# Encoder step on one core: last attention values earlier, output weights split over the first output rows, first two pairs of the up stage by turns

## The chip, the core and the metric

One Trainium2 chip, one core. The metric is the device time of one execution in microseconds. Each kernel is timed several times on a chip and the median is taken. A profiled execution gives a trace of every instruction beside it.

## What is computed

One inference step of a one-layer encoder. 1024 prompt positions and 8 samples of 16 positions make 1152 rows of width 1024, all in float32. In short:

```python
h = rmsnorm(x, g_pre_mix)
qa, ka, va, qb, kb, vb, ga, gb = project(h, w_in)
...
merged = jax.nn.sigmoid(ga) * (oa @ w_oa) + jax.nn.sigmoid(gb) * (ob @ w_ob)
x = x + rmsnorm(merged @ w_out, g_post_mix)
f, conv_new = conv_ffn(rmsnorm(x, g_pre_ffn), conv_buf, w_upg, conv_w, conv_b, w_down)
x = x + rmsnorm(f, g_post_ffn)
```

`oa` and `ob` are two windowed attentions. `conv_ffn` multiplies by `w_upg` (the up projection, 2 x 3072 columns), runs a causal convolution of width 3 and a GELU over one half, multiplies by the other half and by `w_down`.

## The kernel before, in words

Each float32 matrix product is made of three reduced-precision ones: an operand is split into a high part (a copy with rounding, on ACT) and a low part (the difference, on DVE or POOL), and high x high, high x low and low x high are summed in PSUM. An operand's high part is so ready before its low part, and PE can start on it with the matmuls that need the high part alone.

The program is a sequence of stages on PE: projections (0 to 297 us of the span), attention with the remaining projection columns spread between its steps (297 to 601), merge of the two branches with `w_o` (601 to 706), output projection `w_out` with both norms (706 to 816), up stage (816 to 1366), down stage (1372 to the end). The order of the work within a stage is that of the code, moved by a scheduler that places instructions by priority as their inputs become ready; a pool of `bufs=n` buffers makes the next tile wait for the last reader of the tile that had its place. Each engine then runs its own list in order, and SP's list issues the DMAs.

**End of attention** (L840 to L882). Column blocks of the projection are cut in pieces of four steps, a step being 6 matmuls ("dense", L117 to L119, tiles d). What is left at the end runs around the last transposes and `values(prev)`, the last product of attention with V, whose result goes through `oo` and DRAM to the merge's operands `oT` (L901 loads, L902 ACT's high part, L903 DVE's low part). The merge's first matmul is mp (L926). Its result per group g of columns is merged on DVE (L937, mm), split on ACT (L938, mT0h to mT2h) and POOL (L939).

**Output projection** (L985 on). Eight weight tiles wt0 to wt7 are split (L101 ACT, L104 DVE). Nine blocks of 128 rows follow in the order 8, 0 to 7. A block is 48 matmuls (L1060 to L1062, r), then norm, residual and norm (L1068 to L1075, result h), and transposes into the up stage's right operands (L1044 tp, copied out at L1050 or L1048). The blocks' transposes are kept in a list `pending` and run two blocks late; two are left at the end.

**Up stage** (L143 products; right operands xob, xot). 24 pairs f of a column block of the first half and one of the second. It is a scheme with seven products per pair instead of eight; a product is two chunks of 12 matmuls of 128x288, 24 in all, accumulated in a pair of banks x, y or z. For the first five pairs two of the seven products run ahead ("away", banks xh): h11 with right operand b11, then h12 with b21. The left operands come from the raw weights uw by sums on DVE (L127 to L133) and `split_left` (L1019 ACT, L1020 DVE; tiles a, s, h). `split_left` counts its calls with `turn`, 0 to 167, and takes one of two pools by the count:

```python
sp = (wop[1] if next(turn) % 3 else wop[0]).tile([P, 2, 4, P], F32R, name=name, tag="wop")
```

Pool wopa has one buffer and wopb two, so three buffers are used in rotation. ACT also copies results out of PSUM (L1110, L1158), DVE adds and runs the convolution (L1184 to L1220, L1197 the taps), POOL makes the last products (L1216, L1221), and SP stores them to z_dr (L1217, L1218, L1222, L1223).

**Down stage.** Its raw operands z12r, z14r, z16r (L1295, from z_dr) and wd12r and so on (L1296) take places that the up stage leaves. They are split at L1304 (ACT, zap, zs, wbp) and L1305 (DVE). The first matmul is p20s at L1366.

Of the kernel before, what the change touches and what calls it, by code (L numbers as in the profile page):

```python
# [11 lines left out]
F32 = mybir.dt.float32  # L12
# [6 lines left out]
P = 128  # L19
# [33 lines left out]
def encoder_step(ctx, tc, x, w_in, w_o, w_out, w_upg, w_down, kc, vc, state_conv, conv_w, conv_b,  # L53
# [23 lines left out]
    def bcast_row(pool, vec, n, name):  # L77
        t = pool.tile([P, n], F32, name=name)
        nc.sync.dma_start(t[:], bass.AP(tensor=vec.tensor, offset=vec.offset, ap=[[0, P], [1, n]]))
        return t  # L80
# [69 lines left out]
    def banks(pool, name):  # L150
        return [pool.tile([P, 512], F32, name=f"{name}_{c}", tag="ps")[:, 0:CW] for c in range(2)]
# [8 lines left out]
    with ExitStack() as ph:  # L160
# [61 lines left out]
        class Away:  # L222
# [9 lines left out]
            def run(self, i, c):  # L232
                if i == 0:
                    self.ps[c] = self.pool.tile([P, 512], F32, name=f"ixh{self.f}_{c}", tag="ps")[:, 0:CW]
                order = ((0, 0), (1, 0), (0, 1)) if self.early else ((0, 0), (0, 1), (1, 0))
                chunk_product(self.ps[c], self.left[i], of(rf[("b11", "b21")[i]]), c, i == 0, i == 1, order)
# [252 lines left out]
    with ExitStack() as ph:  # L489
# [347 lines left out]
        for u in range(8):  # L837
# [36 lines left out]
                prev = st  # L874
            for _ in dense:
                pass
        run(pieces[0])
        for _ in transposes(prev):
            pass
        run(pieces[1])  # L880
        values(prev)
        run(*pieces[2:])  # L882
    xk_stack.close()
    r1 = [r1_stack.enter_context(tc.tile_pool(name=f"r1{i}", bufs=1, reuse_waits="tile")) for i in range(4)]
    r2 = r2_stack.enter_context(tc.tile_pool(name="r2", bufs=2, reuse_waits="tile"))
# [99 lines left out]
    with ExitStack() as ph:  # L985
        psr = ph.enter_context(tc.tile_pool(name="psr3", bufs=3, space=PSUM, reuse_waits="tile"))
        pst = ph.enter_context(tc.tile_pool(name="pst3", bufs=2, space=PSUM, reuse_waits="tile"))
        xp = ph.enter_context(tc.tile_pool(name="xp3", bufs=2, reuse_waits="tile"))
        gp = ph.enter_context(tc.tile_pool(name="gp3", bufs=1, reuse_waits="tile"))
        gpm = bcast_row(gp, g_post_mix, D, "gpm")  # L990
        gpf = bcast_row(gp, g_pre_ffn, D, "gpf")
        gp.tile([P, 768], F32, name="gap")
        wp = ph.enter_context(tc.tile_pool(name="wp3", bufs=1, reuse_waits="tile"))
        wo = [wp.tile([P, 2, D], F32R, name=f"wt{k}") for k in reversed(range(KD))][::-1]
        for k in range(KD):
            raw = (wr if k % 4 > 1 else wr2).tile([P, D], F32, name=f"wt{k}r", tag="wr")
            nc.sync.dma_start(raw[:], w_out[k])
            split_w(raw, wo[k], "scalar", "vector")
        wr_stack.close()
        uraw = xo_stack.enter_context(tc.tile_pool(name="uraw", bufs=2, side="right", reuse_waits="tile"))  # L1000
        operand("b11")
        wop_a = xo_stack.enter_context(tc.tile_pool(name="wopa", bufs=1, side="right", reuse_waits="tile"))
        wop = [wop_a]

        bq = [[None, None], [None, None]]
        for h, q in ((0, 0), (0, 1), (1, 0), (1, 1)):
            bq[h][q] = r1[2 * h + q].tile([P, 2, 4, CW], F32, name=f"bq{h}{q}", tag="act")

        def up_weights(f, n=2):
            raw = uraw.tile([P, 2, KD, P], F32, name=f"uw{f}{n}", tag="uw")  # L1010
            for i in range(n):
                nc.sync.dma_start(raw[:, i], w_upg[i * NF + f])
            return raw

        turn = iter(range(7 * NF + 2 * NH))

        def split_left(src, name):
            sp = (wop[1] if next(turn) % 3 else wop[0]).tile([P, 2, 4, P], F32R, name=name, tag="wop")
            nc.scalar.activation(sp[:, 0], src, AF.Copy)  # L1019
            nc.vector.tensor_tensor(sp[:, 1], src, fr(sp[:, 0]), op=ALU.subtract)  # L1020
            return sp

        uraws = {f: up_weights(f, 1) for f in range(2)}
        early_op = {}

        def pieces(tb):

            t0, h = (tb * P, 0) if tb < NT - 1 else (H1, 0)
            done = 0
            while done < P:  # L1030
                t = t0 + done
                if tb < NT - 1 and t >= H1:
                    h, t = 1, t - H1
                n = min(P - done, CW - t % CW)
                if tb < NT - 1 and h == 0:
                    n = min(n, H1 - t)
                yield done, h, t // CW, t % CW, n
                done += n

        def transpose_block(src, tb):  # L1040
            for q in range(2):
                pt = pst.tile([P, 4, P], F32, name=f"tp{tb}_{q}", tag="pt")
                for k in range(4):
                    nc.tensor.transpose(pt[:, k], src[:, (4 * q + k) * P:(4 * q + k + 1) * P], ident[:])  # L1044
                for r, h, c, c0, n in pieces(tb):
                    dst = bq[h][q][:, c, :, c0:c0 + n]
                    if q and i < 7:
                        nc.vector.tensor_copy(dst, pt[:, :, r:r + n])  # L1048
                    else:
                        nc.scalar.activation(dst, pt[:, :, r:r + n], AF.Copy)  # L1050

        pending = []
        for i, tb in enumerate(order):
            g, c = tb // 3, (tb % 3) * P
            ps = psr.tile([P, 2, 512], F32, name=f"r{tb}", tag="r")
            for k in range(KD):
                mh, ml = mT[g][0][:, k, c:c + P], mT[g][1][:, k, c:c + P]
                for h in range(2):
                    hs = slice(h * 512, (h + 1) * 512)
                    nc.tensor.matmul(ps[:, h], mh, wo[k][:, 0, hs], start=k == 0, stop=False)  # L1060
                    nc.tensor.matmul(ps[:, h], mh, wo[k][:, 1, hs], start=False, stop=False)
                    nc.tensor.matmul(ps[:, h], ml, wo[k][:, 0, hs], start=False, stop=k == KD - 1)  # L1062
            xt = xp.tile([P, D], F32, name=f"xr{tb}", tag="xt")
            nc.sync.dma_start(xt[:], x[tb])
            st = xp.tile([P, 4], F32, name=f"str{tb}", tag="st")
            r2v = ps[:].rearrange("p a b -> p (a b)")
            h2 = xp.tile([P, D], F32, name=f"h2{tb}", tag="h2", bufs=3)
            nc.scalar.activation(h2[:], r2v, AF.Square, accum_out=st[:, 0:1])  # L1068
            rstd_of(st[:, 0:1], st[:, 1:2])
            nc.vector.scalar_tensor_tensor(h2[:], r2v, st[:, 1:2], gpm[:], op0=ALU.mult, op1=ALU.mult)  # L1070
            nc.vector.tensor_tensor(xt[:], xt[:], h2[:], op=ALU.add)
            nc.sync.dma_start(x1_dr[tb][:], xt[:])
            nc.scalar.activation(h2[:], xt[:], AF.Square, accum_out=st[:, 2:3])
            rstd_of(st[:, 2:3], st[:, 3:4])
            nc.vector.scalar_tensor_tensor(h2[:], xt[:], st[:, 3:4], gpf[:], op0=ALU.mult, op1=ALU.mult)  # L1075
            pending.append((h2, tb))
            while i >= 3 and len(pending) > 2:
                transpose_block(*pending.pop(0))
            if i == 6:
                for c in range(2):  # L1080
                    split_chunk("b11", bq[0][0], c, nc.vector)
                early_op[0] = split_left(uraws[0][:, 0, 0:4], "h11_0")
        for p in pending:
            transpose_block(*p)
    r2_stack.close()


    (b11, b21), (b12, b22) = bq
    wop.append(xo_stack.enter_context(tc.tile_pool(name="wopb", bufs=2, side="right", reuse_waits="tile")))
    pa = xo_stack.enter_context(tc.tile_pool(name="pa", bufs=4, side="right", reuse_waits="tile"))  # L1090
    for name in ("b21", "t3", "t2", "t1", "b22", "t4"):
        operand(name)
# [3 lines left out]
    with ExitStack() as ph:  # L1096
# [23 lines left out]
            product(yb, next(ops), of("b21"), True, True)  # L1120
            return ops, xb, a, yb

        def head_away(f):

            raw = uraws.pop(f, None) or up_weights(f, 1)
            xb = banks(psx, f"xh{f}")
            product(xb, early_op.pop(f, None) or split_left(raw[:, 0, 0:4], f"h11_{f}"), of("b11"), True, False)
            a = snap(xb, [pa.tile([P, CW], F32, name=f"ah{f}_{c}", tag="a")[:] for c in range(2)])
            for c in range(2):
                nc.sync.dma_start(a_dr[f][:, c], a[c])  # L1130
            product(xb, split_left(raw[:, 0, 4:8], f"h12_{f}"), of("b21"), False, True)
            o = [pa.tile([P, CW], F32, name=f"ch{f}_{c}", tag="a") for c in range(2)]
            snap(xb, [t[:] for t in o])
            for c in range(2):
                nc.sync.dma_start(c_dr[f][:, c], o[c][:])

        def head_back(f):
            a = [pa.tile([P, CW], F32, name=f"a{f}_{c}", tag="a")[:] for c in range(2)]
# [111 lines left out]
        forms = right_factors()  # L1250
        next(forms)
        for f in range(NH):
            head_away(f)
            if f in (1, 2):
                next(forms)
        for f in range(NF):
# [323 lines left out]
```

## Time and profile before

| | us |
|---|---|
| median of 3 runs | 1643.92 (1643.70 to 1643.96) |
| profiled execution | 1648.29 |
| its span in the trace | 1646.5 |
| stage r, 706 to 816.3 | 110.3 |
| start of the up stage, 816.3 to 855 | 38.7 |
| rest of the up stage, 855 to 1360 | 505.0 |

The span runs from the first to the last instruction of the trace; the profiled execution's time is 1.8 us longer and 4.4 us over the median. Engines: PE matmuls, PEld weight loads (beside PE), DVE, ACT, POOL, SP (DMA issues). In a row of the timeline stand the start, the duration of the group, engine, line, operation, out<-in, shape and count, and in brackets the idle time before it and what ended that. Names have no buffer numbers there. A group's matmuls overlap, so its duration is a little longer than its share of the pitch.

### The profile page before, as it was taken

The numbers are of one execution on the slowest core, as the hardware profiler recorded it, in microseconds if no ns is written. First come the engines' busy times: TensorE is split into PE (matmuls) and PEld (weight loads), VectorE is DVE, ScalarE is ACT, GpSimd is POOL, SyncE is SP. The second block draws the span as 40 slices with busy tenths as digits, with TensorE's granted clock in tenths as the row PEclk, the third lists the DMA queues.
The fourth block names the chain that finished last, engine by engine and source line by source line (L and its number), as shares of the span: only waits on it lengthen the run. The fifth ranks groups of instructions, "written<-read, shape, count | busy, mean of one in ns | idle before, by whom it ended". The sixth has DMA issues, their size and how long they took to land. (4 is left out here: it accounts for less than half of the span.)

```text
span 1646.5 us, 27860 instructions
## 1 busy us (share of the span) xinstructions
PE 1591.7 (97%) x10887; PEld 1471.5 (89%) x10887; DVE 1096.0 (67%) x2015; ACT 726.1 (44%) x1411; POOL 215.9 (13%) x293
## 2 busy tenths in 40 slices
PE   6999999999999999999999999999999998999997
PEld 5999999878788889978799999999999997888886
DVE  6965544677777746353597866667666665966986
ACT  7611233566555544332373344444444444534342
POOL 1000000221110004310002311122111110000004
PEclk9999999999999999999999999999999999999999
DMA  7743321664543155342164312212212228053023
GB/s 257 250 166 136 119 95 73 215 183 146 167 152 102 60 198 183 120 166 90 67 205 139 106 66 81 69 67 81 81 66 81 75 80 314 1 215 110 1 100 130
DMA packets 93636, 206.47 MB, mean 125 GB/s; under 512 B 19464, under 2 KB 43320, under 8 KB 93504
## 3 DMA queue, kind: packets, MB, share of 16 engines
q1 hardware_dynamic: 93504, 204.69, 36.4%
q8 instruction: 85, 1.39, 0.3%
q14 instruction: 47, 0.39, 0.1%
HBM read 148.13 MB, written 61.24 MB: 127 GB/s over the span
## 5 line engine op out<-in xcount | busy, mean ns | idle before, releaser
L143 PE MATMUL x<-xot,s 128*128 128x288 f32 x1152 | 157.7, 295 | 1.5 <-DVE w L1156 1.5
L143 PEld LDWEIGHTS x<-xot,s 128*128 128x128 f32 x1152 | 154.9, 188 | 1.7 <-ACT a L1019 1.7
L1366 PE MATMUL x<-wbp,zap 128*128 128x512 f32 x576 | 135.3, 389 | 0.0
L1366 PEld LDWEIGHTS x<-wbp,zap 128*128 128x128 f32 x576 | 108.1, 188 | 22.5
L1366 PE MATMUL p<-wbp,zap 128*128 128x512 f32 x432 | 102.4, 394 | 0.0
L1019 ACT ACTIVATE s<-uw 128x512 fp32r<-128x512 f32 x96 | 60.1, 627 | 94.6 <-issue 42.0
L671 ACT ACTIVATE p<-p,m 128x256 f32<-128x256 f32 (+4 forms) x128 | 74.8, 586 | 56.5 <-DVE m L666 56.5
L1366 PEld LDWEIGHTS p<-wbp,zap 128*128 128x128 f32 x432 | 82.4, 191 | 17.3
L1020 DVE TENSOR_TENSOR s<-uw,s 128x512 fp32r<-128x512 f32 x96 | 70.1, 730 | 34.0 <-ACT s L1019 34.0
L1197 DVE SCALAR_TENSOR_TENSOR wk<-w,cw,wk 128x128 f32<-128x128 f32 (+2 forms) x144 | 83.2, 614 | 7.4 <-ACT wk L1195 6.6
L1020 DVE TENSOR_TENSOR a<-uw,a 128x512 fp32r<-128x512 f32 x62 | 42.9, 693 | 63.3 <-ACT a L1019 62.0
L143 PE MATMUL x<-xob,s 128*128 128x288 f32 x576 | 81.1, 295 | 3.2 <-ACT wk L1195 1.4
L143 PEld LDWEIGHTS x<-xob,s 128*128 128x128 f32 x576 | 78.1, 188 | 3.8 <-ACT wk L1195 1.6
L143 PE MATMUL z<-xot,s 128*128 128x288 f32 x576 | 80.7, 295 | 0.0
L143 PE MATMUL z<-xot,a 128*128 128x288 f32 x576 | 80.7, 295 | 0.0
L143 PE MATMUL ix<-t,s_i 128*128 128x288 f32 x576 | 78.6, 295 | 0.3 <-DVE iu L188 0.3
L143 PEld LDWEIGHTS z<-xot,s 128*128 128x128 f32 x576 | 78.1, 188 | 0.0
L143 PEld LDWEIGHTS z<-xot,a 128*128 128x128 f32 x576 | 78.1, 188 | 0.0
L143 PEld LDWEIGHTS ix<-t,s_i 128*128 128x128 f32 x576 | 77.2, 188 | 0.5 <-issue 0.5
L173 ACT ACTIVATE s_i<-iw 128x512 fp32r<-128x512 f32 x48 | 30.3, 630 | 88.4 <-PE ix L143 49.0
L143 PE MATMUL x<-xob,a 128*128 128x288 f32 x456 | 63.9, 295 | 0.0
L143 PE MATMUL y<-xob,a 128*128 128x288 f32 x456 | 63.9, 295 | 0.0
(625 smaller groups left out, 3828.2 us busy)
## 6 DMA issues: line engine op xcount, KB each, us to landing
uw<-in_w_upg SPq DMA_DIRECT2D x53, 512.0 KB, 4.4
iw<-in_w_in SPq DMA_DIRECT2D x31, 512.0 KB, 4.6
gg<-in_dr SPq DMA_DIRECT2D x16, 576.0 KB, 3.7
z_dr<-wk SPq DMA_DIRECT2D x24, 256.0 KB, 2.1
in_dr<-gt SPq DMA_DIRECT2D x30, 192.0 KB, 1.9
z_dr<-wk SPq DMA_DIRECT2D x24, 224.0 KB, 1.9
xt<-in_x SPq DMA_DIRECT2D x9, 512.0 KB, 10.1
oT<-o_dr SPq DMA_DIRECT2D x8, 576.0 KB, 5.3
```

Source lines behind the costliest of these rows:

```text
L143: nc.tensor.matmul(ps, w[:, i, k], right(j, c, k), start=first and n == 0, stop=last and n == len(todo) - 1, skip_group_check=True)
L173: nc.scalar.activation(sp[:, 0], src, AF.Copy)
L671: nc.scalar.activation(p[h][:, 0:n], p[h][:, 0:n], AF.Exp, bias=least[h], scale=-1.0, accum_out=st.d[:, h, i:i + 1])
L1019: nc.scalar.activation(sp[:, 0], src, AF.Copy)
L1020: nc.vector.tensor_tensor(sp[:, 1], src, fr(sp[:, 0]), op=ALU.subtract)
L1197: nc.vector.scalar_tensor_tensor(out, src(t), cw[:, f, t:t + 1], out, op0=ALU.mult, op1=ALU.add)
L1366: nc.tensor.matmul(ps, z[:, i, k, c], w[:, j, k], start=first and n == 0, stop=last and n == 2, skip_group_check=True)
```

## The change

Three edits are named. In the end of the attention, the left-over dense pieces become one stream, and the transposes come after 4 steps of it and `values(prev)` after 2 more, so that the values stand 12 matmuls earlier. In the output projection the weights lie in two pools of four tiles, one ahead of the x and norm pools and one behind, and their splits get a priority that is higher by 200. In the up stage the first two pairs run by turns (pair 0 b11, pair 1 b11, pair 0 b21, pair 1 b21; class `Away`), both of their first left operands are split after output block 6, and the last block of rows takes the transposes of both pending blocks in among its own matmuls (at k = 1 and 6), so that one block's transposes are left at the end.

The diff does a fourth thing: the left operands' pools are both made early, with one buffer each, and the rule that picks between them stays.

```diff
--- before.py
+++ after.py
@@ -874,12 +874,16 @@
                 prev = st
             for _ in dense:
                 pass
-        run(pieces[0])
+        rest = stream(pieces)
+        for _ in zip(range(4), rest):
+            pass
         for _ in transposes(prev):
             pass
-        run(pieces[1])
+        for _ in zip(range(2), rest):
+            pass
         values(prev)
-        run(*pieces[2:])
+        for _ in rest:
+            pass
     xk_stack.close()
     r1 = [r1_stack.enter_context(tc.tile_pool(name=f"r1{i}", bufs=1, reuse_waits="tile")) for i in range(4)]
     r2 = r2_stack.enter_context(tc.tile_pool(name="r2", bufs=2, reuse_waits="tile"))
@@ -985,22 +989,26 @@
     with ExitStack() as ph:
         psr = ph.enter_context(tc.tile_pool(name="psr3", bufs=3, space=PSUM, reuse_waits="tile"))
         pst = ph.enter_context(tc.tile_pool(name="pst3", bufs=2, space=PSUM, reuse_waits="tile"))
-        xp = ph.enter_context(tc.tile_pool(name="xp3", bufs=2, reuse_waits="tile"))
-        gp = ph.enter_context(tc.tile_pool(name="gp3", bufs=1, reuse_waits="tile"))
-        gpm = bcast_row(gp, g_post_mix, D, "gpm")
-        gpf = bcast_row(gp, g_pre_ffn, D, "gpf")
-        gp.tile([P, 768], F32, name="gap")
-        wp = ph.enter_context(tc.tile_pool(name="wp3", bufs=1, reuse_waits="tile"))
-        wo = [wp.tile([P, 2, D], F32R, name=f"wt{k}") for k in reversed(range(KD))][::-1]
+
+        wo = []
+        for i in range(2):
+            wp = ph.enter_context(tc.tile_pool(name=f"wp3{i}", bufs=1, reuse_waits="tile"))
+            wo += [wp.tile([P, 2, D], F32R, name=f"wt{4 * i + k}") for k in range(4)]
+            if i == 0:
+                xp = ph.enter_context(tc.tile_pool(name="xp3", bufs=2, reuse_waits="tile"))
+                gp = ph.enter_context(tc.tile_pool(name="gp3", bufs=1, reuse_waits="tile"))
+                gpm = bcast_row(gp, g_post_mix, D, "gpm")
+                gpf = bcast_row(gp, g_pre_ffn, D, "gpf")
         for k in range(KD):
             raw = (wr if k % 4 > 1 else wr2).tile([P, D], F32, name=f"wt{k}r", tag="wr")
             nc.sync.dma_start(raw[:], w_out[k])
-            split_w(raw, wo[k], "scalar", "vector")
+            with tc.high_priority(offset=200):
+                split_w(raw, wo[k], "scalar", "vector")
         wr_stack.close()
         uraw = xo_stack.enter_context(tc.tile_pool(name="uraw", bufs=2, side="right", reuse_waits="tile"))
         operand("b11")
-        wop_a = xo_stack.enter_context(tc.tile_pool(name="wopa", bufs=1, side="right", reuse_waits="tile"))
-        wop = [wop_a]
+        wop = [xo_stack.enter_context(tc.tile_pool(name=f"wop{i}", bufs=1, side="right", reuse_waits="tile"))
+               for i in range(2)]
 
         bq = [[None, None], [None, None]]
         for h, q in ((0, 0), (0, 1), (1, 0), (1, 1)):
@@ -1054,6 +1062,8 @@
             g, c = tb // 3, (tb % 3) * P
             ps = psr.tile([P, 2, 512], F32, name=f"r{tb}", tag="r")
             for k in range(KD):
+                if i == 8 and k in (1, 6):
+                    transpose_block(*pending.pop(0))
                 mh, ml = mT[g][0][:, k, c:c + P], mT[g][1][:, k, c:c + P]
                 for h in range(2):
                     hs = slice(h * 512, (h + 1) * 512)
@@ -1074,19 +1084,19 @@
             rstd_of(st[:, 2:3], st[:, 3:4])
             nc.vector.scalar_tensor_tensor(h2[:], xt[:], st[:, 3:4], gpf[:], op0=ALU.mult, op1=ALU.mult)
             pending.append((h2, tb))
-            while i >= 3 and len(pending) > 2:
+            while 3 <= i < 8 and len(pending) > 2:
                 transpose_block(*pending.pop(0))
             if i == 6:
                 for c in range(2):
                     split_chunk("b11", bq[0][0], c, nc.vector)
-                early_op[0] = split_left(uraws[0][:, 0, 0:4], "h11_0")
+                for f in range(2):
+                    early_op[f, 0] = split_left(uraws[f][:, 0, 0:4], f"h10_{f}")
         for p in pending:
             transpose_block(*p)
     r2_stack.close()
 
 
     (b11, b21), (b12, b22) = bq
-    wop.append(xo_stack.enter_context(tc.tile_pool(name="wopb", bufs=2, side="right", reuse_waits="tile")))
     pa = xo_stack.enter_context(tc.tile_pool(name="pa", bufs=4, side="right", reuse_waits="tile"))
     for name in ("b21", "t3", "t2", "t1", "b22", "t4"):
         operand(name)
@@ -1120,19 +1130,21 @@
             product(yb, next(ops), of("b21"), True, True)
             return ops, xb, a, yb
 
-        def head_away(f):
-
-            raw = uraws.pop(f, None) or up_weights(f, 1)
-            xb = banks(psx, f"xh{f}")
-            product(xb, early_op.pop(f, None) or split_left(raw[:, 0, 0:4], f"h11_{f}"), of("b11"), True, False)
-            a = snap(xb, [pa.tile([P, CW], F32, name=f"ah{f}_{c}", tag="a")[:] for c in range(2)])
-            for c in range(2):
-                nc.sync.dma_start(a_dr[f][:, c], a[c])
-            product(xb, split_left(raw[:, 0, 4:8], f"h12_{f}"), of("b21"), False, True)
-            o = [pa.tile([P, CW], F32, name=f"ch{f}_{c}", tag="a") for c in range(2)]
-            snap(xb, [t[:] for t in o])
-            for c in range(2):
-                nc.sync.dma_start(c_dr[f][:, c], o[c][:])
+        class Away:
+
+
+            def __init__(self, f):
+                self.f, self.raw = f, uraws.pop(f, None) or up_weights(f, 1)
+                self.xb = banks(psx, f"xh{f}")
+
+            def run(self, i):
+                f = self.f
+                left = early_op.pop((f, i), None) or split_left(self.raw[:, 0, 4 * i:4 * i + 4], f"h1{i}_{f}")
+                product(self.xb, left, of(("b11", "b21")[i]), i == 0, i == 1)
+                out = [pa.tile([P, CW], F32, name=f"{'ac'[i]}h{f}_{c}", tag="a") for c in range(2)]
+                snap(self.xb, [t[:] for t in out])
+                for c in range(2):
+                    nc.sync.dma_start((a_dr, c_dr)[i][f][:, c], out[c][:])
 
         def head_back(f):
             a = [pa.tile([P, CW], F32, name=f"a{f}_{c}", tag="a")[:] for c in range(2)]
@@ -1250,7 +1262,15 @@
         forms = right_factors()
         next(forms)
         for f in range(NH):
-            head_away(f)
+            if f > 1:
+                first = Away(f)
+                first.run(0)
+                first.run(1)
+            elif f:
+                both = [Away(0), Away(1)]
+                for i in range(2):
+                    for e in both:
+                        e.run(i)
             if f in (1, 2):
                 next(forms)
         for f in range(NF):
```

The instruction lists show the places. On ACT around the end of the merge (mT is the merge's result, wt the output weights), before:

```order
L938 ACTIVATE mT2h<-mm_2_0_8274 128x384
L938 ACTIVATE mT0h<-mm_0_0_8289 128x384
L938 ACTIVATE mT1h<-mm_1_0_8304 128x384
L101 ACTIVATE wt_8394<-wt0r 128x1024
L101 ACTIVATE wt_8393<-wt1r 128x1024
L101 ACTIVATE wt_8392<-wt2r 128x1024
```

and after:

```order
L942 ACTIVATE mT2h<-mm_2_0_8274 128x384
L942 ACTIVATE mT0h<-mm_0_0_8289 128x384
L101 ACTIVATE wt_8376<-wt0r 128x1024
L101 ACTIVATE wt_8377<-wt1r 128x1024
L101 ACTIVATE wt_8378<-wt2r 128x1024
L101 ACTIVATE wt_8379<-wt3r 128x1024
L942 ACTIVATE mT1h<-mm_1_0_8304 128x384
L101 ACTIVATE wt_8393<-wt4r 128x1024
```

The four tiles of the first pool now stand ahead of the last group's copy mT1h; line numbers are 4 higher there.

On PE in the up stage, pair 6 (a and s are left operands, xob and xot right ones, x, y and z banks; each line is one of the two chunks), before:

```order
L143 MATMUL y_0_10796<-xob_9151,a_6_10798 128x288 x12
L143 MATMUL y_1_10797<-xob_9151,a_6_10798 128x288 x12
L143 MATMUL z_0_10825<-xot_9155,s_6_10828 128x288 x12
L143 MATMUL z_1_10826<-xot_9155,s_6_10828 128x288 x12
L143 MATMUL x_0_10763<-xot_9159,s_6_10856 128x288 x12
L143 MATMUL x_1_10764<-xot_9159,s_6_10856 128x288 x12
L143 MATMUL x_0_10763<-xot_9163,s_6_10888 128x288 x12
L143 MATMUL x_1_10764<-xot_9163,s_6_10888 128x288 x12
```

and after:

```order
L143 MATMUL y_0_10799<-xob_9157,a_6_10801 128x288 x12
L143 MATMUL y_1_10800<-xob_9157,a_6_10801 128x288 x12
L143 MATMUL z_0_10828<-xot_9161,s_6_10831 128x288 x2
L143 MATMUL z_1_10829<-xot_9161,s_6_10831 128x288 x2
L143 MATMUL z_0_10828<-xot_9161,s_6_10831 128x288 x10
L143 MATMUL z_1_10829<-xot_9161,s_6_10831 128x288 x10
L143 MATMUL x_0_10766<-xot_9165,s_6_10859 128x288 x12
L143 MATMUL x_1_10767<-xot_9165,s_6_10859 128x288 x12
L143 MATMUL x_0_10766<-xot_9169,s_6_10891 128x288 x12
L143 MATMUL x_1_10767<-xot_9169,s_6_10891 128x288 x12
L143 MATMUL z_0_10828<-xot_9177,a_6_10967 128x288 x8
L143 MATMUL x_0_10766<-xob_9173,s_6_10934 128x288 x2
```

The products are the same and in the same order at large, but some chunks are broken: two matmuls of each chunk, which use the left operand's high part alone, and the other ten later, or eight matmuls of the following z product ahead of the last x product.

On SP at the end of the up stage (z_dr stores of the last pair, raw operands of the down stage), before:

```order
L1295 DMA z12r<-z_dr_9194 128x1152
L1296 DMA wd12r<-in_w_down 128x1024
L1295 DMA z12r<-z_dr_9195 128x1152
L1259 DMA out<-st 128x432
L1296 DMA wd12r<-in_w_down 128x1024
L1296 DMA wd14r<-in_w_down 128x1024
L1222 DMA z_dr_9205<-wk 128x448
L1217 DMA z_dr_9205<-wk 128x64
L1218 DMA z_dr_9205<-wk 128x512
L1223 DMA z_dr_9205<-wk 128x128
```

and after:

```order
L1279 DMA out<-st 128x432
L1315 DMA z12r<-z_dr_9200 128x1152
L1316 DMA wd12r<-in_w_down 128x1024
L1229 DMA z_dr_9211<-wk 128x64
L1230 DMA z_dr_9211<-wk 128x512
L1234 DMA z_dr_9211<-wk 128x448
L1235 DMA z_dr_9211<-wk 128x128
L1315 DMA z12r<-z_dr_9201 128x1152
L1316 DMA wd12r<-in_w_down 128x1024
```

The second z12r and second wd12r now stand behind the four stores of the last pair; before, they stood ahead of them.

## The prediction

> **What bounds the kernel now.** I read the page's busy shares first, then the windows of the stages after the attention, then what PE waited for, then single instructions at the places of the change.
>
> ```profile
> span 1646.5 us, 27860 instructions
> PE 1591.7 (97%) x10887; PEld 1471.5 (89%) x10887; DVE 1096.0 (67%) x2015; ACT 726.1 (44%) x1411; POOL 215.9 (13%) x293
> ```
>
> ```profile
> 706.00:816.30 110.30, 107.55 (x482) 88.25 (x483) 49.57 (x60) 32.87 (x53) 10.58 (x18) 0.97 0.30 105
> 816.30:855.00 38.70, 35.44 (x266) 34.57 (x265) 34.87 (x37) 29.04 (x52) 1.88 (x4) 1.00 0.58 179
> 855.00:1360.00 505.00, 500.33 (x3748) 499.47 (x3747) 351.29 (x574) 225.25 (x429) 98.58 (x139) 1.00 0.26 85
> ```
>
> ```profile
> PE p20s L1366 <- ACT wbp L1304: 5.8, 1, 5.8
> PE r L1060 <- ACT wt L101: 2.8, 1, 2.8
> PE mp L926 <- ACT oT L902: 2.6, 1, 2.6
> PE xh L143 <- ACT h L1019: 2.0, 1, 2.0
> PE x L143 <- ACT s L1019: 1.2, 1, 1.2
> PE tp L1044 <- ACT bq L1050: 1.0, 1, 1.0
> PE tp L1044 <- DVE h L1075: 0.3, 1, 0.3
> ```
>
> PE is the bound. Columns of the windows: length, then busy time of PE, PEld, DVE, ACT, POOL, then granted clock. From 855 to 1360 PE idles 4.7 us in 505 at full clock, so whatever holds PE there lengthens the program by itself. The waits are the seams: into the merge (mp), the output projection (r), the up stage (tp, xh; 0.96 + 1.95 + 0.35 = 3.3 us) and the down stage (p20s).
>
> **Edit not in the change's name: left-operand buffers, three to two.** Before, the rule "second pool if the turn modulo 3 isn't 0" picks between a pool of one buffer and a pool of two. After, both pools hold one, and the rule is the same. So turns go A B B A B B: each turn that leaves 2 modulo 3 takes the buffer that the product directly before it still reads, and its ACT split cannot start until that product's last matmul. The turns run 0 to 167; 56 are of this kind. PE's program then takes two forms. Without filler (30 after the heads): 2+2 matmuls on the high part, and 10+10 after the low part. With filler (23): 8 or 6 matmuls of the neighbouring product stand ahead. The three others are in the heads, costed below.
>
> ```profile
> 1116.48 3.36 PE L143 MATMUL z<-xot,a 128*128 128x288 f32 x24
> 1119.68 3.36 PE L143 MATMUL x<-xob,a 128*128 128x288 f32 x24
> ```
>
> ```profile
> 1116.68 0.41 ACT L1158 ACTIVATE w<-x 128x288 f32<-128x288 f32 x1 [1.19 <-PE x L143]
> 1116.99 0.62 ACT L1019 ACTIVATE a<-uw 128x512 fp32r<-128x512 f32 x1
> 1119.88 0.64 ACT L1019 ACTIVATE s<-uw 128x512 fp32r<-128x512 f32 x1 [1.51 <-PE z L143]
> ```
>
> ```profile
> 1117.64 0.69 DVE L1020 TENSOR_TENSOR a<-uw,a 128x512 fp32r<-128x512 f32 x1 [1.06 <-ACT a L1019]
> 1105.25 1.81 DVE L1197 SCALAR_TENSOR_TENSOR wk<-w,cw,wk 128x448 f32<-128x448 f32 x4
> ```
>
> ```profile
> 824.46 1.32 PE L143 MATMUL xh<-xob,h 128*128 128x288 f32 x8 [1.95 <-ACT h L1019]
> ```
>
> Products of 24 matmuls start 3.20 us apart (0.133 each) and last 3.36, so they overlap by 0.16. The price without filler: the product ends at 1119.84 and ACT starts the split it released at 1119.88 (0.04); the split takes 0.63 and PE follows in 0.06 (as at 824.46, after ACT's first copy of that group). The next product starts 3.36 + 0.73 = 4.09 after its forerunner in place of 3.20: 0.89 lost. The restart adds 0.1 (the 8 matmuls at 824.46 took 1.32, against 8 x 0.133 + 0.16 = 1.23). Four matmuls fill 0.53 us, then PE needs the low part: DVE starts 0.03 after ACT's end (1117.61 to 1117.64) and takes 0.69, so about 0.2 more is missing. That is 1.2. In places one of ACT's copies stands ahead (L1158 to L1019 is 0.31 apart), or a DVE instruction is under way (L1197's four hold DVE for 1.81; half of one is 0.23). I take 1.4; ends 1.0 (the low part always in time) and 1.9 (ACT's copy and 0.4 of DVE each time). 29 x 1.4 = **41 us** (29 to 55); the thirtieth is turn 167, in the seam below. With filler: 6 to 8 matmuls cover 0.8 to 1.06 us, about the 0.73 that the high part needs; what stays is the low part, 0 to 0.4. 23 x 0.2 = **4.6** (0 to 9).
>
> **Values moved up.**
>
> ```profile
> 601.19 0.49 ACT L540 ACTIVATE gt<-d 128x384 f32<-128x384 f32 x1 [6.20 <-PE d L119]
> 601.58 1.05 ACT L101 ACTIVATE wo1s<-wo1r 128x1024 fp32r<-128x1024 f32 x1
> 602.53 2.21 ACT L902 ACTIVATE oT<-oT 128x1152 fp32r<-128x1152 f32 x2
> ```
>
> The first mp waits for ACT's oT split, which stands right behind the last dense copy and wo1's split without a gap. The values move by 12 matmuls, but the last dense matmul and ACT's order after it stay. **0** (a gain of at most 2.6, all of this wait; a loss of the same 0.3 as one ACT hand-over).
>
> **Output weights.**
>
> ```profile
> 705.16 0.53 ACT L938 ACTIVATE mT0h<-mm 128x384 fp32r<-128x384 f32 x1 [1.55 <-DVE mm L937]
> 707.64 1.04 ACT L101 ACTIVATE wt<-wt0r 128x1024 fp32r<-128x1024 f32 x1
> ```
>
> ```profile
> 708.73 0.79 PE L1060 MATMUL r<-wt,mT2h 128*128 128x512 f32 x1 [2.77 <-ACT wt L101]
> 714.87 0.40 PE L1060 MATMUL r<-wt,mT2h 128*128 128x512 f32 x1
> 715.11 0.39 PE L1061 MATMUL r<-wt,mT2h 128*128 128x512 f32 x1
> ```
>
> ```profile
> 709.00:715.00 6.00, 6.00 (x15) 4.51 (x16) 4.99 (x5) 3.58 (x4) 0.00 (x0) 0.51 0.63 206
> ```
>
> wt0 to wt3 now take the place of oT0 to oT3, whose last reader is the merge's end, and stand ahead of mT1h on ACT. The first split can then start at about 705.7 (end of mT0h) and end at 706.7; PE's first row follows at 706.8 in place of 708.73. Before, PE issued 14 r matmuls (0.24 apart at full clock, 714.87 to 715.11) between 705.96, where its 2.77 of idle began, and 714.87: 8.9 us for 14 x 0.24 = 3.3 of work, so the seam costs 5.6: 2.8 idle and 2.8 at half clock. After: 0.84 idle, and about 0.85 for wt0's low part, whose DVE instruction stands behind the merge: 1.7. I take **-4** (5.6 less 1.7), the half clock gone with the long idle (ends -4.5 and -1, where it stays). The Trainium skill, "TensorE: Matmul & The Clock Gate", "What's actually happening", has the clock halved after an idle window of about 3.4 us; by it 2.77 us would not reach that, and only the idle would be saved, about -1. The trace disagrees: 0.51 follows 2.77 idle.
>
> **Up start.** The transposes of the two pending blocks go into the last r block, and pairs 0 and 1 run b11, b11, b21, b21. 47 matmuls (x 0.133 + 0.16 = 6.4, with 0.1 for the start 6.5 us) now stand ahead of the last transposes.
>
> ```profile
> 816.39 1.02 ACT L1068 ACTIVATE h<-r 128x1024 f32<-128x1024 f32 x1 [6.14 <-PE r L1062]
> ```
>
> ```profile
> 818.43 1.28 DVE L1070 SCALAR_TENSOR_TENSOR h<-r,str,gpm 128x1024 f32<-128x1024 f32 x1 [0.73 <-POOL str L97]
> 820.89 1.22 DVE L1071 TENSOR_TENSOR xr<-xr,h 128x1024 f32<-128x1024 f32 x1
> 822.03 2.62 DVE L983 TENSOR_TENSOR xob<-bq,xob 128x1152 fp32r<-128x1152 f32 x2
> 825.75 1.29 DVE L1075 SCALAR_TENSOR_TENSOR h<-xr,str,gpf 128x1024 f32<-128x1024 f32 x1 [0.44 <-POOL str L97]
> ```
>
> The last block's norm on DVE has three operand splits of 1.31 between its steps now: 0.04 (a hand-over as at 1119.84) + 2.04 (816.39 to 818.43) + 1.28 + 1.31 + 1.22 + 1.31 + 1.31 + 1.29 = 9.8 us after r's end. PE's cover is 6.5, so it idles 3.3. Then come the heads' shared turns 2, 5 and 8; in PE's order, which moves neighbours between them, the products of turns 4, 7 and 8 end up directly behind the last reader of their buffer: 1.4, 1.8 (both copies ahead) and 1.2, by the price above. 7.7 against 3.3: **+4.4** (2 to 7).
>
> **Seam to the down stage.**
>
> ```profile
> 1359.20 0.43 SPq L1295 DMA_DIRECT2D z12r<-z_dr  x1
> 1364.15 0.43 SPq L1296 DMA_DIRECT2D wd12r<-in_w_down  x1
> 1371.04 0.42 SPq L1223 DMA_DIRECT2D z_dr<-wk  x1
> ```
>
> ```profile
> 1372.06 0.80 PE L1366 MATMUL p20s<-wbp,zs 128*128 128x512 f32 x1 [5.82 <-ACT wbp L1304]
> ```
>
> ```profile
> 1366.49 1.06 ACT L1304 ACTIVATE zap<-z12r 128x1024 fp32r<-128x1024 f32 x1 [2.10 <-DMA z12r<-z_dr]
> 1370.95 1.06 ACT L1304 ACTIVATE wbp<-wd12r 128x1024 fp32r<-128x1024 f32 x1 [2.22 <-DMA wd12r<-in_w_down]
> ```
>
> z12r lies on the raw up weights, which the last product's split (turn 167, no filler) still reads. PE's last product ended at 1366.24 (1372.06 less 5.82). Call E the end of the one before it, 3.20 earlier: 1363.04. The first p20s came at E + 9.0. Before, that split was done long before E and both z12r were issued by 1359.63. After, it ends at E + 1.4. On SP the four z_dr stores of the last pair now stand ahead of the second z12r and wd12r: the last product ends at E + 4.5 and those stores are out about 3.8 to 4.8 later (1371.04 is 4.8 after PE's end at 1366.24), so wd12r goes at about E + 8.7. It took 6.8 to land (1364.15 to 1370.95), the split 1.06, often two of them: p20s at E + 16.5 to 17.5. **+8** (6 to 9).
>
> **Sum.** 41 + 4.6 + 0 - 4 + 4.4 + 8 = **+54**. The profiled execution took 1648.29 us, 1.8 around its span and 4.4 above the median 1643.92; it would be 1702, the median 1698. All low ends: 29 + 0 - 4.5 + 2 + 6 = 32.5, so 1676. All high ends: 55 + 9 + 0 - 1 + 7 + 9 = 79, so 1723.
>
> **Rivals.** *Cover holds (faster, 0.05).* The waits for the two buffers vanish if the split of a shared buffer finishes inside matmuls already queued. That decides at 1.45 us of cover (0.04 + 0.63 + 0.03 + 0.69 + 0.06) behind each shared product; then only the seams remain: -4 and -3.3, so 1637. For it: 23 of 53 have 0.8 to 1.06 of cover. Against: 30 have none, in PE's own order.
> *The clock falls (slower still, 0.09).* Each idle costs a stretch at half clock as at 709, 2.8 us: 29 x 2.8 = 81 more, so 1779. For: 2.77 idle was enough there. Against: 816.3 to 855 lost 3.3 us in three pieces and stayed at 1.00. The Trainium skill, same page, "A second HAM failure mode: psum-queue depth-cycling", describes a kernel whose short idles between groups of matmuls made the clock swing; no row here shows that for idles near 1 us.
> *DVE is late (0.15, inside the forecast's range).* Each low part waits behind a whole pass: 1.9 each, 29 x 0.5 = 15 more, 1713.
> *No effect (0.04).* The scheduler's turns cancel what each seam gains: within 3 us of 1644.
>
> **Chances.** The forecast has 0.67, with DVE late 0.82. The range 1676 to 1723 holds these. About 0.2% (3 us) is what a measurement of this kernel tells from none: faster 0.05, same 0.04, slower 0.91.
>
> **What would show it.** ACT's L1019 group would have idle before it released by PE's products, and PE waits on ACT s, a L1019 would rise from 1.2 to some 30 us with 0.6 to 1.2 each, on DVE L1020 to about 10; the granted clock in the up stage stays 1.00. r's wait falls under 1 us without 0.51 behind it; mp's wait stays at 2.6; the last transposes wait about 3.3; p20s waits 12 to 13. The forecast is wrong if PE's idle in the up stage stays under 15 us, or if the clock there falls.

## The result and the profile after

The changed kernel takes 1720.47 us (median of 4 runs, 1718.79 to 1725.67), the kernel before 1643.94 in the same session: a ratio of 1.0467, 95% interval 1.0441 to 1.0493, or 76.5 us slower. The forecast was 1698, with a range of 1676 to 1723, so the result lies 2.5 below the upper end. The profiled execution took 1721.64 us, 73.4 more than that of before (1648.29).

First the page of the changed kernel: its span, and the busy time of each engine.

```profile
span 1719.9 us, 27829 instructions
PE 1618.6 (94%) x10887; PEld 1476.7 (86%) x10887; DVE 1098.1 (64%) x2015; ACT 727.9 (42%) x1411; POOL 216.0 (13%) x293
```

The counts of PE, DVE, ACT and POOL are those of before, and the busy times of DVE, ACT and POOL are within about 2 us of them; PE is busy 27 us longer and idle 101 us in place of 55. The work is the same and it waits more. What PE waited for in the changed kernel (us in total, times, longest):

```profile
PE x L143 <- ACT s L1027: 14.5, 17, 1.0
...
PE p20s L1386 <- ACT wbp L1324: 11.6, 1, 11.6
PE y L143 <- DVE a L1028: 10.3, 12, 1.4
PE y L143 <- ACT a L1027: 6.1, 6, 1.0
PE z L143 <- ACT s L1027: 5.1, 7, 0.8
PE xh L143 <- ACT h L1027: 4.4, 3, 1.6
...
PE mp L930 <- ACT oT L906: 2.6, 1, 2.6
...
PE tp L1052 <- DVE h L1085: 1.9, 1, 1.9
PE xh L143 <- DVE h L1080: 1.9, 1, 1.9
...
PE r L1070 <- ACT wt L101: 0.7, 1, 0.7
```

The waits of x, y and z for the left operands a and s (L1027 is ACT's high part, L1028 DVE's low part) were 1.2 us in all before. The wait at p20s has doubled, the one at r fell from 2.8 to 0.7, and mp's is what it was. The stages in windows: the stretch, its length, the busy time of PE, PEld, DVE, ACT and POOL, the granted clock, and last the share and rate of the DMA engines. The second window is the start of the up stage, with the products that run ahead; the third is the rest of the stage, called the tails here.

```profile
705.00:813.50 108.50, 107.23 (x498) 87.66 (x499) 52.76 (x62) 34.72 (x59) 11.44 (x18) 1.00 0.33 121
813.50:852.00 38.50, 29.78 (x201) 28.04 (x200) 33.45 (x35) 28.62 (x46) 6.67 (x7) 0.96 0.49 158
852.00:1433.00 581.00, 539.47 (x3840) 518.82 (x3840) 354.76 (x579) 230.43 (x433) 91.95 (x137) 0.99 0.24 80
```

From the first and last instructions of each stage in both traces, the 73.4 us divide so: up to the merge's first matmul -1.8 (601.96 against 603.73, of which 1.1 was there before the attention began and the rest by 354, in both cases far ahead of the first changed code); merge and wait for the output weights -2.0; first output row to the first product of the tails +9.2 (705.01 to 860.37, before 708.73 to 854.86); tails +61.1 (to 1432.88, before to 1366.24); wait at p20s +5.8; down stage +1.0.

How one turn of the tails loses time is seen on PE. The changed kernel, from 1002 on:

```profile
1002.26 3.36 PE L143 MATMUL x<-xob,a 128*128 128x288 f32 x24
1006.64 0.80 PE L143 MATMUL y<-xob,a 128*128 128x288 f32 x4 [1.02 <-ACT a L1027]
1007.27 0.42 PE L143 MATMUL z<-xot,s 128*128 128x288 f32 x2
1009.14 2.92 PE L143 MATMUL y<-xob,a 128*128 128x288 f32 x20 [1.44 <-DVE a L1028]
1011.90 3.09 PE L143 MATMUL z<-xot,s 128*128 128x288 f32 x22
1014.83 3.36 PE L143 MATMUL x<-xot,s 128*128 128x288 f32 x24
1019.20 3.66 PE L143 MATMUL x<-xot,s 128*128 128x288 f32 x24 [1.02 <-ACT s L1027]
1022.70 0.56 PE L143 MATMUL x<-xob,s 128*128 128x288 f32 x3
```

At a pitch of 3.20, y would start at 1005.46; it starts 1.18 later, behind ACT's split. It runs four matmuls on the high part, z slips two in, then PE stands for the low part. The next x starts at 1014.83 and not two pitches after 1006.64, which is 1.79 more. So this turn cost 2.97. The x at 1019.20 is a plain one, a turn without filler whose low part is in time: 1.17 late, and 0.30 more to its successor, 1.47.

### The profile page after: what moved, and what is told of

Read it like the earlier page. It is cut to its first block, busy times and chain, and to the rows that moved or that the text cites. A ratio compares the mean times of both kernels' runs of the same rounds, so it can differ in the third digit from the quotient of the medians.

```text
span 1719.9 us, 27829 instructions
## 1 busy us (share of the span) xinstructions
PE 1618.6 (94%) x10887; PEld 1476.7 (86%) x10887; DVE 1098.1 (64%) x2015; ACT 727.9 (42%) x1411; POOL 216.0 (13%) x293
## 3 DMA queue, kind: packets, MB, share of 16 engines
q8 instruction: 85, 1.39, 0.3%
## 5 line engine op out<-in xcount | busy, mean ns | idle before, releaser
L143 PE MATMUL x<-xot,s 128*128 128x288 f32 x1152 | 165.8, 300 | 16.8 <-ACT s L1027 14.5
L1027 ACT ACTIVATE s<-uw 128x512 fp32r<-128x512 f32 x96 | 60.5, 630 | 133.6 <-PE y L143 62.3
L1028 DVE TENSOR_TENSOR s<-uw,s 128x512 fp32r<-128x512 f32 x96 | 75.2, 784 | 58.1 <-ACT s L1027 56.4
L143 PE MATMUL z<-xot,s 128*128 128x288 f32 x576 | 84.6, 297 | 5.9 <-ACT s L1027 5.1
L143 PE MATMUL z<-xot,a 128*128 128x288 f32 x576 | 85.6, 298 | 1.3 <-ACT a L1027 1.1
L143 PE MATMUL y<-xob,a 128*128 128x288 f32 x456 | 71.3, 304 | 16.4 <-DVE a L1028 10.3
L1209 DVE SCALAR_TENSOR_TENSOR wk<-w,cw,wk 128x128 f32<-128x128 f32 (+2 forms) x144 | 84.1, 612 | 3.7 <-ACT wk L1207 2.4
L143 PEld LDWEIGHTS y<-xob,a 128*128 128x128 f32 x456 | 64.2, 192 | 20.6 <-DVE a L1028 13.1
L1028 DVE TENSOR_TENSOR a<-uw,a 128x512 fp32r<-128x512 f32 x62 | 49.6, 799 | 41.9 <-ACT a L1027 40.4
L143 PE MATMUL x<-xob,a 128*128 128x288 f32 x456 | 67.7, 297 | 0.7 <-DVE a L1028 0.7
```

The costliest lines, as they stand in the source:

```text
L143: nc.tensor.matmul(ps, w[:, i, k], right(j, c, k), start=first and n == 0, stop=last and n == len(todo) - 1, skip_group_check=True)
L1209: nc.vector.scalar_tensor_tensor(out, src(t), cw[:, f, t:t + 1], out, op0=ALU.mult, op1=ALU.add)
```

## The experiments

The median of the kernel before was 1646.11, 1646.14 and 1647.78 us in the three sessions; ratios are to the runs of the same session.

**1. Two buffers alone.** The kernel before, with nothing changed but the second pool.

```diff
-    wop.append(xo_stack.enter_context(tc.tile_pool(name="wopb", bufs=2, side="right", reuse_waits="tile")))
+    wop.append(xo_stack.enter_context(tc.tile_pool(name="wopb", bufs=1, side="right", reuse_waits="tile")))
```

> The kernel before with one edit: the second pool of left operands has one buffer in place of two; all else, the seams too, as before. Theory (two buffers, used A B B): the tails of the up stage lose what they lost in the changed kernel, 46 (forecast) to 60 us (its trace), and the seam to the down stage 6 to 8: 1695 to 1715. Rival (the loss comes from the pairs by turns and the transposes moved into the last row block, with the clock): within 5 us of 1644.

Measured: 1726.99 us, ratio 1.048 (1.0462 to 1.0498), 81 us slower and 12 over the theory's upper end, which had left out the shared turns at the stage's start (xh waits 6.4 us for ACT's h there, before 2.0) and any half clock (five spells of 3.4 us between 823 and 1019 in its trace, 8.5 us lost, where before has none). Its waits on PE:

```profile
PE x L143 <- ACT s L1019: 13.8, 16, 1.0
...
PE p20s L1366 <- ACT wbp L1304: 11.2, 1, 11.2
PE y L143 <- DVE a L1020: 10.3, 12, 1.5
```

They are those of the changed kernel, in a kernel with none of the three named parts. The loss comes from the buffers alone.

**2. Three buffers in the changed kernel.** A third pool, made where the second stood before.

```diff
-            sp = (wop[1] if next(turn) % 3 else wop[0]).tile([P, 2, 4, P], F32R, name=name, tag="wop")
+            sp = wop[next(turn) % 3].tile([P, 2, 4, P], F32R, name=name, tag="wop")
...
     (b11, b21), (b12, b22) = bq
+    wop.append(xo_stack.enter_context(tc.tile_pool(name="wop2", bufs=1, side="right", reuse_waits="tile")))
```

> The changed kernel with a third left-operand buffer, made where the second pool stood before, and the three used in rotation. Theory: the tails are as before, PE's waits there under 6 us, p20s waits 5.8 again; what is left is -4 at the output weights and some 1 to 4 more idle at the start of the up stage: 1640 to 1645. Rival (the turns of the pairs cost it): 1690 or more.

Measured: 1645.41 us, ratio 0.9996 (0.9985 to 1.0006). PE's waits from 813 us on:

```profile
PE x L143 <- DVE wk L1169: 4.7, 3, 2.8
PE p20s L1387 <- ACT wbp L1325: 4.4, 1, 4.4
PE xh L143 <- DVE h L1080: 1.9, 1, 1.9
```

No wait for a left operand is left. With the buffer back, all three named parts together are worth nothing that can be measured.

**3. Two buffers, strictly by turns.** The changed kernel, with another rule.

```diff
-            sp = (wop[1] if next(turn) % 3 else wop[0]).tile([P, 2, 4, P], F32R, name=name, tag="wop")
+            sp = wop[next(turn) % 2].tile([P, 2, 4, P], F32R, name=name, tag="wop")
```

> The changed kernel with its two buffers, the rule modulo 2 in place of modulo 3: A B A B. Theory (what costs is the use of one buffer twice running, not that there are two): a split has the whole product ahead, 3.2 us, for its 1.45: the tails lose under 5 us, only the seam's stores ahead of the last loads stay (6 us): 1645 to 1655. Rival (two buffers are too few in any order): 1690 or more.

Measured: 1653.74 us, ratio 1.0039 (1.0024 to 1.0054). There is no wait for a left operand in the tails, with two buffers. What is left against the second experiment is 8.3 us, and the traces put it at one place:

```profile
PE p20s L1386 <- ACT wbp L1324: 12.7, 1, 12.7
```

12.7 against 4.4 is 8.3. That the two figures agree to a tenth is chance, since this wait is 2.8 to 5.9 us in the six traces with three buffers and 10.6 to 12.7 in the six with two. Here SP's list has the four z_dr stores ahead of the last loads, as in the changed kernel; in the second experiment it has the order of before. So not the number of buffers but the rule made for three cost the tails their time, and the seam is a price of its own.

**4. Values and output weights, on the kernel before.** These two parts of the diff as they stand, and nothing else.

> The kernel before with two of the three named parts: values moved up and output weights split in two pools; the start of the up stage and three buffers as before. Theory: -4 at the first output rows, 0 for the values: 1638 to 1641, with no half clock behind the first row's wait. Rival (the clock falls at this seam all the same): 1642 to 1644.

Measured: 1640.65 us, ratio 0.9969 (0.9954 to 0.9983), inside the expected range; its trace has no half clock behind the first row's wait.

**5 and 6. Each of the two alone.**

> The kernel before with the output weights' two pools and priority alone. Theory: PE's wait at the first output row falls from 2.8 to 0.7, with 1.2 for low parts behind it; 1 to 4 us faster than before (the half clock behind that wait came in one trace of before's code and not in another, so it may be no part of the gain). Rival (what the two parts together gained came from the values): 0.

Measured, weights alone: 1643.01 us, ratio 0.9986 (0.9975 to 0.9998), 2.3 us faster, with 0.7 of wait at the first row and 0.9 for the low parts.

> The kernel before with the last values moved up alone. Theory: the merge's first matmul still waits 2.6 for ACT's split behind the last dense copy: 0, within 0.1%. Rival: up to 2.6 us faster.

Measured, values alone: 1645.48 us, ratio 0.9997 (0.9986 to 1.0008); mp waits 2.6 as ever. The gain of the fourth is the weights', as far as one of these intervals can tell from another; the values give nothing.

**7. By turns, the transposes left where they were.** The second experiment's kernel, with the moved transposes put back.

```diff
-                if i == 8 and k in (1, 6):
-                    transpose_block(*pending.pop(0))
...
-            while 3 <= i < 8 and len(pending) > 2:
+            while i >= 3 and len(pending) > 2:
```

> The changed kernel with three buffers (as in the second experiment), the pairs by turns, but the transposes of the two pending blocks left behind the last output block, as before. Theory (by turns and moved transposes are worth about nothing, either way): within 2 us of that experiment, 1643 to 1648, the first transposes waiting 1.0 for ACT again and the last ones none. Rival (moving the transposes is what cost the 5 us between that experiment and the fourth): 1639 to 1642.

Measured: 1641.48 us, ratio 0.9971 (0.996 to 0.9982). That is the rival's number: it was the moved transposes that gave back what the weights had gained. The trace of the second experiment shows how:

```profile
813.81 1.74 PE L143 MATMUL xh<-xob,h 128*128 128x288 f32 x12
817.45 5.78 PE L143 MATMUL xh<-xob,h 128*128 128x288 f32 x30 [1.90 <-DVE h L1080]
823.64 1.07 PE L1052 MATMUL tp<-ident,h 128*128 128x128 f32 x8 [0.41 <-DVE h L1085]
```

With no transposes behind the last output block, xh starts at once; its second chunk waits for L1080, the DVE pass that reads the last block's result r out of PSUM. The transposes had covered that time. After it this trace has 1.7 us of half clock (granted 0.53 from 817.30 to 820.40, 0.92 in the 3.1 us behind); the seventh's trace has neither, and goes from its first output row to the first product of the tails in 143.2 us, against 146.3. One execution each; the medians differ by 3.9.

**8. The sums on POOL.** The changed kernel, with the four sums of a pair (L127 to L133) on POOL in the tails.

```diff
-    def left_factors(raw, ahead, name, part):
+    def left_factors(raw, ahead, name, part, sums=nc.vector):
...
-        nc.vector.tensor_tensor(a11, a11, a21, op=ALU.subtract)
+        sums.tensor_tensor(a11, a11, a21, op=ALU.subtract)
```

> The changed kernel, two buffers, with the four sums of a pair's left operands in the tails on POOL in place of DVE. Theory (in one of four products without filler the low part stands behind two of these sums on DVE, which makes its price 3.0 in place of 1.4): y's waits for DVE a, 10.3 us in twelve, fall under 4; 5 to 12 us faster than the changed kernel, if POOL's sums are in time. Rival (the lateness is of another source): those waits stay at 10.

Measured: 1752.41 us, ratio 1.0647 (1.063 to 1.0664). Its waits on PE:

```profile
PE x L143 <- ACT s L1027: 29.1, 18, 2.7
...
PE y L143 <- DVE a L1028: 1.0, 6, 0.2
```

The wait that was to go went, from 10.3 to 1.0, which fits the sums on DVE as what made the low part late. But y's waits for the high part rose from 6.1 to 11.0 and x's doubled, so this run alone does not prove it; the rows of DVE below show it directly. The kernel became 32 us slower than the changed one, where 5 to 12 faster was expected. ACT's waits for the first two sums rose only from 13.8 us (on DVE) to 19.7 (on POOL). DVE itself became slower: its L1209 passes, the convolution, took 850 ns on average in the tails, in the changed kernel 618, and ACT's waits for them rose from 17.4 to 62.7 us.

**9 and 10. Other numbers of repeats.** Two buffers, with rules that repeat 27 and 84 times in 168 turns, in place of 56.

```diff
-            sp = (wop[1] if next(turn) % 3 else wop[0]).tile([P, 2, 4, P], F32R, name=name, tag="wop")
+            t = next(turn)
+            sp = wop[(t + t // 6) % 2].tile([P, 2, 4, P], F32R, name=name, tag="wop")
```

For 84 the index is `t // 2 % 2`.

> The changed kernel with its two buffers by turns, but every sixth turn the same one again: 27 turns that take the buffer of the product before, in place of 56 (changed kernel) and 0 (third experiment). Theory (each such turn has its own price): from 1653.7 and 1720.5 the price is 66.8 / 56 = 1.19 us a turn: 1654 + 27 x 1.19 = 1686, with 5 either way for where in a pair they fall. Rival (a few such turns are enough to upset the clock or the order of the whole stage): above 1705; rival (only those that fall on certain products cost): under 1670.

> The changed kernel with its two buffers in the order A A B B: 84 turns that take the buffer of the product before. Theory (a price for each): 1654 + 84 x 1.19 = 1754, with 12 either way. Rival (the loss levels off, since ACT, DVE and PE fall into step): under 1735.

Measured: 1691.52 us, ratio 1.0267 (1.0236 to 1.0298), just over the expected 1681 to 1691, and 1738.19 us, ratio 1.0552 (1.0522 to 1.0582), between the theory's 1742 and the rival's 1735. Above the third experiment's 1.0039, and by 1646 us, that is 37.5 us for 27 repeats, 70.4 for the changed kernel's 56 and 84.4 for 84: 1.39, 1.26 and 1.00 a repeat. Against an equal price for each, 84 is 16 us short and 27 somewhat over.

Filler does not explain this. In the instruction lists the repeats of the tails with matmuls of a neighbour in front are 11 of 26, 22 of 53 and 33 of 79, the same share each time. It does set the price of a single turn, as the forecast had it: in all three traces most turns with filler cost 0.2 to 0.3 us, and the commonest price without it is 1.2 to 1.5. What differs is the y turn whose low part comes late. Behind the same wait of 1.02 for the high part it waits 1.44 more in the changed kernel (six times), 0.5 with 27 repeats (four times, and shorter waits elsewhere), and nothing with 84 (nine times). PE's waits of y, first with 27 repeats and then with 84, where no line of y for DVE is left:

```profile
PE y L143 <- DVE a L1029: 4.1, 10, 0.5
PE y L143 <- ACT a L1028: 4.1, 4, 1.0
```

```profile
PE y L143 <- ACT a L1028: 9.2, 9, 1.0
```

Nine times 1.44 is 13 us, an estimate of most of the 16. Why 27 repeats cost more each stays open; the half clock between the output projection and the seam is no reason, for each of the three traces has four spells of 3.4 us there.

## Why the prediction was right, point by point

**Two buffers in the tails: the mechanism right, the size a quarter short.** Forecast 41 + 4.6 and, inside the seam's term, 1.3 for turn 167; measured +61.1. (The forecast counted 30 turns without filler and 23 with; the lists have 31 and 22.) The pattern of the changed kernel repeats after 21 products. One period:

```profile
985.66 3.70 PE L143 MATMUL z<-xot,s 128*128 128x288 f32 x24 [0.72 <-ACT s L1027]
...
1060.97 1.30 PE L143 MATMUL z<-xot,s 128*128 128x288 f32 x6 [0.72 <-ACT s L1027]
```

75.31 us, and 21 x 3.20 is 67.2: 8.1 lost, where the forecast had 4 x 1.4 + 3 x 0.2 = 6.2. From the starts of the products within it: the four turns without filler cost 1.28, 2.97, 1.47 and 1.23, 1.74 on average in place of 1.4; the three with filler 0.26, 0.17 and 0.26, where 0.2 was forecast; and 0.47 falls on a neighbour whose low part comes late. The mis-sized step is the low part of one turn in four, for which the forecast had "half of one" DVE instruction. DVE, POOL and ACT ahead of the y at 1006.64:

```profile
1004.58 1.70 DVE L1028 TENSOR_TENSOR s<-uw,s 128x512 fp32r<-128x512 f32 x1
1006.20 1.69 DVE L131 TENSOR_TENSOR uw<-uw 128x512 f32<-128x512 f32 x1
1007.81 0.68 DVE L129 TENSOR_TENSOR uw<-uw 128x512 f32<-128x512 f32 x1
1008.41 0.68 DVE L1028 TENSOR_TENSOR a<-uw,a 128x512 fp32r<-128x512 f32 x1
```

```profile
1004.02 1.71 POOL L1233 TENSOR_TENSOR wk<-wk,w 128x576 f32<-128x576 f32 x1 [2.90 <-DVE w L1232]
1005.69 1.65 POOL L1228 TENSOR_TENSOR wk<-wk,w 128x576 f32<-128x576 f32 x1
```

```profile
1005.66 0.41 ACT L1120 ACTIVATE a<-x 128x288 f32<-128x288 f32 x1 [0.27 <-PE x L143]
1005.96 0.62 ACT L1027 ACTIVATE a<-uw 128x512 fp32r<-128x512 f32 x1
```

ACT's high part ends at 1006.58, one copy late as priced. DVE could follow at 1006.61 and follows at 1008.41: two sums stand ahead, and one of them takes 1.69 in place of 0.68. The eighth experiment takes the two sums away, and the wait is gone there. This was the rival "DVE is late", true in one turn of four; its price was given as 1.9 for all, and this turn took 2.97.

**The half clock: a little.** The rival had 2.8 us for each idle. Granted clock in the tails of the changed kernel was below full in two spells, from 921 to 925 and here:

```profile
1085.40:1088.80 3.40, 3.40 (x17) 3.40 (x16) 0.46 (x1) 0.00 (x0) 0.00 (x0) 0.54 0.00 0
```

By length times what is missing of full clock, these cost 3.4 us in all, and the spells at 845 to 858 another 3.4. So the rival was there behind a few pairs of idles close together (0.77 and 1.71, 1.02 and 1.44, 1.62 and 1.51), and not behind the rest: the pair of 1.02 and 1.44 stands six times in the tails and was followed by a spell once. The forecast had named a falling clock in the up stage as a sign of being wrong; it fell, for 6.8 of the 76 us.

**Output weights: -4, more than the runs bear out.** The wait went to 0.74 and the low parts cost 1.2, near the 0.84 and 0.85 worked out. The weights alone gained 2.3 (0.3 to 4.1). The idle saved, less the low parts, is only 2.8 - 0.7 - 1.2 = 0.9. The step that was too sure is "the half clock gone with the long idle", worth a full 2.8 by one trace. Here are the same 6.8 us in the kernel before, in the first experiment and in the sixth; in all three this code is the same and PE waits 2.8 at the same place:

```profile
708.40:711.80 3.40, 3.07 (x7) 2.34 (x8) 3.09 (x3) 3.12 (x4) 0.41 (x1) 0.50 0.23 75
711.80:715.20 3.40, 3.40 (x10) 2.59 (x9) 2.39 (x3) 1.06 (x1) 0.00 (x0) 0.55 0.94 312
```

```profile
708.40:711.80 3.40, 3.09 (x12) 2.26 (x13) 3.40 (x3) 2.82 (x3) 0.09 (x1) 1.00 0.30 86
711.80:715.20 3.40, 3.40 (x16) 2.79 (x16) 2.27 (x3) 1.06 (x1) 0.00 (x0) 1.00 0.83 290
```

```profile
708.40:711.80 3.40, 2.10 (x6) 1.43 (x7) 2.41 (x3) 3.40 (x5) 0.99 (x1) 0.85 0.17 10
711.80:715.20 3.40, 3.40 (x11) 2.63 (x11) 2.23 (x2) 1.24 (x2) 0.00 (x0) 0.64 0.78 294
```

Half clock after this wait cost some 3 us in the first execution, nothing in the second and 1.7 in the third. None of the nine traces with the shorter wait has any there. The three average 1.6 us; with the 0.9 of idle that makes 2.5, an estimate near the 2.3 measured. So the half clock is probably a part of the gain, but as a chance and not as a price; 0.9 alone would lie inside the interval too. One trace of before could not show that.

**Values: 0, right.** mp waits 2.62 in the changed kernel too, and the sixth experiment finds nothing. (The sums of the low and high ends leave this term out; with its 2.6 the range would begin at 1674.)

**Up start: +4.4, measured more.** PE waited 8.9 us there (1.9, 1.9, 4.4 and 0.7 for low parts) against 3.3: +5.6. The half clock at 845 to 858 added 3.4, so this part cost about 9.0, above the 7 of its upper end. The three turns waited about what was forecast. The last transposes waited 1.9 and not 3.3, because PE had already lost 1.9 ahead of them for the PSUM of the last output block, a wait that the forecast did not have: it took the moved transposes as work and not as cover.

**Seam to the down stage: +8, right.** p20s came at 1444.50; the product before the last ended at 1427.86 (E), so E + 16.6, forecast 16.5 to 17.5, by the path given: stores, then the second z12r and wd12r, then the splits. That it fits so closely is partly luck: wd12r was issued at E + 10.3 and not E + 8.7, and landed 5.1 later and not 6.8. Against the second experiment, the third prices the seam at about 8.

**The sum.** The traces exceed the forecast +54 by 19 us: about 14 lie in the tails and about 5 at the start of the up stage. Both are losses taken too small, and the range held with little to spare.

## What to carry to other kernels

A rule that deals out buffers belongs to their number: with one buffer fewer, "modulo 3" made every third user wait for the user directly before it, while "modulo 2" on the same two buffers cost the loop nothing. Read the small edits of a diff beside its title: here the one that the title leaves out made the whole result. Of the named parts the output weights are worth keeping, and transposes that stand between a stage's end and the next stage's start can be cover: the kernels of the fourth and seventh experiments, 0.3% faster than before, are the best of those run.

## What the runs showed of the hardware

The spells of half clock named above are 3.4 us long or, in the kernel before, 6.8. Whether an idle of 2.6 to 2.8 us sets one off changes from one execution of the same instructions to the next: mp's wait of 2.6 stands in all twelve traces and ten have a spell there, r's wait of 2.8 stands in three and two have one (0.50 granted at first in one, 1.00 in another). The Trainium skill, "TensorE: Matmul & The Clock Gate", "What's actually happening", says that the window of some 3.4 us runs freely and that its phase differs from run to run; these traces agree with that, and by it a forecast should carry such a spell as a chance and not as a price. The whole idle window that the prediction names was not needed here: 2.6 us were enough ten times in twelve.

A sum or difference of 128x512 on DVE took 0.68 us alone and 1.69 or 1.70 when POOL ran a product: the one begun at 1004.58 ended 0.55 after POOL's first product (1005.73), the one at 1006.20 ended 0.55 after its second (1007.34). The Trainium skill, "SBUF — State Buffer", "SBUF: two separate sides", has DVE and POOL share a pair of ports under a lock held for a whole instruction, which a DVE instruction with two inputs in SBUF also needs; these rows agree, and so does the eighth experiment, where L1209's passes on DVE rose from 618 to 850 ns with four more sums per pair on POOL.
